# The mLSTM's scores as two pairs of 64-row matmuls in two banks, without the block-diagonal query tile

## The chip, the core and the metric

The kernel runs on one core of a Trainium2 chip. The metric is the device time of one execution in microseconds. Its engines are called as the profile calls them: PE (TensorE, matmuls; PEld are its weight loads), DVE (VectorE), ACT (ScalarE), POOL (GpSimd), SP (SyncE, which here issues DMAs). Each takes its instructions in the order that the program gives it.

## What is computed

One layer of a hybrid encoder, for 1024 prompt frames and 32 sample frames of width 1024: a combined input projection feeds an mLSTM (4 heads of 64), a forgetting attention ("fox", 8 heads) and a spatial gate; their outputs are concatenated ("mix") and projected; then come a layer norm, a SwiGLU feed-forward and a second norm. The change is in the mLSTM, which goes by chunks. Cut to what matters:

```python
def _mlstm_chunk(carry, inp):
    C0, n0, m0 = carry
    q, k, v, li, lf = inp
    ...
    s = jnp.einsum('bthd,bshd->bhts', q, k) * w_intra
    num = (jnp.einsum('bhts,bshd->bthd', s, v)
           + jnp.einsum('bthk,bhkv->bthv', q, C0) * w_inter.transpose(0, 2, 1)[..., None])
    den = s.sum(-1) + jnp.einsum('bthk,bhk->bht', q, n0) * w_inter
    ...
    h = num / den.transpose(0, 2, 1)[..., None]
```

## The kernel before

Everything is float32. The large products split each operand into a high and a low part and run three matmuls of a faster float32 kind (L130 to L132, L402 to L404); the mLSTM's small products are plain float32 matmuls, each of which shows as two weight loads and two matmul rows in the profile.

The mLSTM goes over 9 chunks (`mlstm(j)`): 8 of 128 prompt frames, and the 32 sample frames as chunk 8. A chunk loads `qk` (tag `mqk`): 128 partitions, on which heads 0 and 2 lie in partitions 0 to 63 and heads 1 and 3 in 64 to 127; columns 0 and 1 of its second axis are the queries of the two head pairs, 2 and 3 their keys. For the scores, a tile `qb` (tag `mqb`, one buffer) holds the queries block-diagonally: POOL sets it to zero (L719), two DMAs bring each head's 64 rows into its own half (L722), and one matmul for each pair contracts over all 128 rows and gives two heads side by side (L746), both pairs in one PSUM bank of the pool `pss` (tag `s`). DVE multiplies the bank by the decay weights `mw` (L748). Then follow the transposed keys (L754, a bank of the pool `pt`, tag `t`), the numerator `nd` (L762), the old state's part (L767), the state's update (L777, L784), a chain of small DVE and ACT steps (L793 to L811), and `to_mix` (L821): two PE transposes, a copy by ACT (L823), and a store to `dmix` in DRAM.

PSUM's eight banks are three `g` for the large products, two `t` for transposes (fox's, the keys', `to_mix`'s) and modulation, two `s` for fox's and the mLSTM's scores, and one `o`.

Chunks 0 to 3 are interleaved with fox heads 0 to 7 and the rest of the input projection, by a written list:

```python
ORDER = "q0 f0 g q1 a f1 a g S q2 f2 k1p s a q3 f3 a v q4 f4 a q5 f5 o a m0 G0 q6 f6 a m1 G1p G2p q7 m2 f7 a m3 G3"
```

Fox and mLSTM stand in it under `tc.high_priority(HPA)`. What each engine gets, and in which order, is set by a planner of the language (`schedule_with_timeline_sim=True`), which puts instructions in the order in which it reckons that their operands and buffers will be ready. After this stretch comes the output projection's first half, "wo0": `wo_mix(0, ...)` loads `dmix` (L1130) k tile by k tile, in the order 2, 3, 4, 6, 7, 5, 0, 1, where 0 and 1 are the mLSTM's; ACT and DVE split them (L1131, L1132); `wo_range` runs 24 matmuls for each of 8 output blocks, and DVE adds each to the residual `z` (L1199), which empties its bank. The first block's `z` is also averaged as a pivot (L1056 to L1058). Chunks 4 to 8 run later, among fox's second half and the feed-forward (`mixers`).

The tag `mqb` serves once more, for `scan` in `gates`, before the chunks.

## Time and profile before

| | |
|---|---|
| time, median of 3 runs | 1345.75 us (1345.29 to 1346.57) |
| span of the profiled execution | 1344.9 us |
| PE busy | 1324.0 us, 98% |
| PEld busy | 1208.3 us, 90% |
| DVE busy | 989.1 us, 74% |
| ACT busy | 655.8 us, 49% |
| POOL busy | 231.9 us, 17% |
| DMA, SP's queue | 49.0% of 16 engines |
| granted PE clock | full in all 40 slices (9 of 9 tenths) |

The page gives the profiled execution's span, and no other time of it; the runs' median lies 0.85 us above that span. In a timeline row stand start and length in us, engine, line, operation, output<-inputs by the program's names, shape and count; a bracket tells how long the engine sat idle before and what ended that. Rows of one kind that follow each other are merged. SPq is the issue of a DMA, not its transfer. A matmul's row begins with its stream and ends when its result is out, so rows overlap; the step from one start to the next is what it takes of PE. "128*128" ahead of a shape are the rows and columns of weights.

### The profile page before, as it was taken

To read this page: it belongs to the slowest core of one execution; us is meant where nothing else is said; L and a number is where in the kernel's file an instruction comes from. 1 tells how busy PE (TensorE), PEld (TensorE's weight loads), DVE (VectorE), ACT (ScalarE), POOL (GpSimd) and SP (SyncE) were. 2 spreads that over 40 slices of the span, in tenths; PEclk is the share of its full clock that TensorE was granted. 3 is DMA by queue.
4 is the path that set the end of the run, shared out by engine and by line. 5 is a ranking of instruction groups with operands and counts; after the bars stand their busy time and mean duration, and the time that the engine had idled before them with its cause. 6 is when DMAs were issued, how large, how long until landed. Compare 5 with 4: busy or idle time off the path is not lost.

```text
span 1344.9 us, 25607 instructions
## 1 busy us (share of the span) xinstructions
PE 1324.0 (98%) x9684; PEld 1208.3 (90%) x9684; DVE 989.1 (74%) x2091; ACT 655.8 (49%) x1305; POOL 231.9 (17%) x263
## 2 busy tenths in 40 slices
PE   9999999999999999999999999999999999999996
PEld 6798888888999888888888888999999999999995
DVE  5635655678779667686876776678979887988777
ACT  3413445455547545545454454435754453635355
POOL 0102100143246100000000001464610000000341
PEclk9999999999999999999999999999999999999999
DMA  9585465546557754454344332663785858554221
GB/s 362 207 299 154 150 204 186 174 131 207 181 195 257 191 136 130 117 163 126 115 121 116 110 104 82 217 175 112 205 231 154 228 148 225 139 175 131 89 79 67
DMA packets 119450, 221.73 MB, mean 165 GB/s; under 512 B 18580, under 2 KB 62768, under 8 KB 119328
## 3 DMA queue, kind: packets, MB, share of 16 engines
q1 hardware_dynamic: 112096, 207.55, 49.0%
q0 software_dynamic: 6032, 11.94, 5.2%
q8 instruction: 76, 1.25, 0.4%
q10 hardware_dynamic: 1200, 0.62, 0.2%
q14 instruction: 46, 0.38, 0.1%
HBM read 188.13 MB, written 51.85 MB: 178 GB/s over the span
## 4 chain that ended last, share of the span: by engine, by line
PE 68%; DVE 4%; DMA 1%; ACT 1%; issue 1%; DVEq 0%; ACTq 0%
PE up_g L130 6%; PE up_g L132 6%; PE up_g L131 6%; PE dn_g L130 4%; PE dn_g L132 4%; PE dn_g L131 4%; PE sup_u L132 3%; PE sup_u L131 3%; PE sup_u L130 3%; PE wo_g L131 2%; PE wo_g L132 2%; PE wo_g L130 2%; PE sup_g L132 2%; PE sup_g L131 2%; PE sup_g L130 2%; PE fox_t L943 2%
## 5 line engine op out<-in xcount | busy, mean ns | idle before, releaser
L130 PE MATMUL up_g<-tm_ah,up_whi 128*128 128x512 f32 (+1 forms) x384 | 140.0, 365 | 0.0
L131 PE MATMUL up_g<-tm_al,up_whi 128*128 128x512 f32 (+1 forms) x384 | 140.0, 365 | 0.0
L132 PE MATMUL up_g<-tm_ah,up_wlo 128*128 128x512 f32 (+1 forms) x384 | 139.7, 364 | 0.0
L1368 ACT CAST sup_whi<-sup_raw 128x1024 fp32r<-128x1024 f32 x54 | 56.1, 1048 | 89.3 <-PE dn_u L131 43.9
L130 PEld LDWEIGHTS up_g<-tm_ah,up_whi 128*128 128x128 f32 x384 | 72.3, 188 | 11.1 <-DVE tm_al L1246 0.4
L132 PEld LDWEIGHTS up_g<-tm_ah,up_wlo 128*128 128x128 f32 x384 | 72.3, 188 | 11.1
L131 PEld LDWEIGHTS up_g<-tm_al,up_whi 128*128 128x128 f32 x384 | 72.3, 188 | 10.7
L916 ACT ACTIVATE fox_p<-fox_s,fox_fmx 128x384 f32<-128x384 f32 (+2 forms) x96 | 55.2, 579 | 53.0 <-DVE fox_fmx L914 41.2
L1199 DVE SCALAR_TENSOR_TENSOR wo_z<-dn_g,start_mod,wo_z 128x512 f32<-128x512 f32 (+4 forms) x120 | 60.3, 521 | 22.6 <-PE dn_g L132 22.0
L118 DVE TENSOR_TENSOR up_wlo<-up_raw,up_whi 128x1024 fp32r<-128x1024 f32 x50 | 65.2, 1305 | 15.0 <-ACT up_whi L117 13.7
L1369 DVE TENSOR_TENSOR sup_wlo<-sup_raw,sup_whi 128x1024 fp32r<-128x1024 f32 x54 | 68.0, 1263 | 10.7 <-ACT sup_whi L1368 10.7
L117 ACT CAST up_whi<-up_raw 128x1024 fp32r<-128x1024 f32 x50 | 52.4, 1048 | 47.2 <-PE up_g L131 23.9
L130 PE MATMUL dn_g<-up_acth,dn_whi 128*128 128x512 f32 (+2 forms) x200 | 73.5, 368 | 0.8 <-DVE wo_z L1199 0.8
L132 PE MATMUL dn_g<-up_acth,dn_wlo 128*128 128x512 f32 (+2 forms) x200 | 73.3, 366 | 0.0
L131 PE MATMUL dn_g<-up_actl,dn_whi 128*128 128x512 f32 (+2 forms) x200 | 72.8, 365 | 0.0
L948 ACT CAST fox_pth<-fox_t 128x512 fp32r<-128x512 f32 (+1 forms) x80 | 41.6, 542 | 59.2 <-PE fox_t L943 57.5
L117 ACT CAST dn_whi<-dn_raw 128x1024 fp32r<-128x1024 f32 (+1 forms) x44 | 42.7, 971 | 51.7 <-PE up_g L131 16.0
L911 DVE TENSOR_REDUCE fox_fmx<-fox_s 128x1 f32<-128x384 f32 (+2 forms) x96 | 52.8, 553 | 16.3 <-PE fox_s L908 15.0
L949 DVE TENSOR_TENSOR fox_ptl<-fox_t,fox_pth 128x512 fp32r<-128x512 f32 (+1 forms) x80 | 49.9, 631 | 15.9 <-ACT fox_pth L948 15.6
L118 DVE TENSOR_TENSOR dn_wlo<-dn_raw,dn_whi 128x1024 fp32r<-128x1024 f32 (+1 forms) x44 | 49.5, 1125 | 10.4 <-ACT dn_whi L117 9.5
L402 PE MATMUL tm_g<-tm_whi,start_h1h 128*128 128x256 f32 (+1 forms) x192 | 55.3, 288 | 0.7 <-DVE tm_traw L477 0.7
L1320 POOL DMA_DIRECT2D start_dp<-w_gu x19 | 19.8, 1067 | 209.0 <-DMA start_dp<-w_gu 209.0
(684 smaller groups left out, 4799.7 us busy)
## 6 DMA issues: line engine op xcount, KB each, us to landing
up_raw<-w_gu SPq DMA_DIRECT2D x50, 512.0 KB
ada_late<-w_ada SPq DMA_DIRECT2D x28, 512.0 KB
dn_raw<-w_dn SPq DMA_DIRECT2D x28, 512.0 KB
sup_raw<-w_gu SPq DMA_DIRECT2D x20, 512.0 KB
start_dp<-w_gu SPq DMA_DIRECT2D x19, 512.0 KB
start_dp<-w_gu POOLq DMA_DIRECT2D x19, 512.0 KB, 8.0
wo_raw<-w_o SPq DMA_DIRECT2D x18, 512.0 KB
sup_raw<-start_dp SPq DMA_DIRECT2D x18, 512.0 KB
```

Source lines behind the costliest of these rows:

```text
L117: nc.scalar.copy(hi[:, :w], raw[:, :w])
L118: (eng or nc.vector).tensor_tensor(lo[:, :w], raw[:, :w], f(hi[:, :w]), ALU.subtract)
L130: nc.tensor.matmul(ps, hi, xh(k), start=start and k == 0, stop=False)
L131: nc.tensor.matmul(ps, hi, xl(k), start=False, stop=False)
L132: self.lastmm = nc.tensor.matmul(ps, lo, xh(k), start=False, stop=stop and k == n - 1)
L402: nc.tensor.matmul(ps[:, :ncol], xh, hi, start=k == 0, stop=False)
L911: nc.vector.tensor_reduce(mxs[:, x:x + 1], s[:, :w], AX.X, ALU.max, negate=True)
L916: nc.scalar.activation(pr[:, lo:hi], banks[x][:, :hi - lo], AF.Exp, bias=mxs[:, 0:1], accum_out=sums[:, x:x + 1])
L949: nc.vector.tensor_tensor(pl[:, :e], ps[:, :e], f(ph[:, :e]), ALU.subtract)
L1199: self.lastz = self.nc.vector.scalar_tensor_tensor(z[:, m, x:y], ps[:, x - a:y - a], g[i], z[:, m, x:y], ALU.mult, ALU.add)
L1368: nc.scalar.copy(h, x)
L1369: tt(l, x, f(h), ALU.subtract)
```

## The change

The tile `qb`, its memset and its two DMAs for each chunk go. Each head's score is now a matmul of its own, contracted over the head's 64 rows: queries and keys of one head lie on the same partitions of `qk`. Heads 0 and 2 (rows 0 to 63) go to a bank of `pss`, heads 1 and 3 (rows 64 to 127) to a bank of `pt`. DVE's product with the weights becomes two, one for each bank. The scan of `gates` gets a tag of its own.

```diff
-        scan = t([R, 2, 192], "mqb")
+        scan = t([R, 2, 192], "mscan")
...
-        qb = t([P, 2, 2, P], "mqb")
-        nc.gpsimd.memset(qb, 0.0)
-        for a in range(2):
-            r = slice(64 * a, 64 * a + 64)
-            self.load(qb[r, :, a, :L], self.dmqk[r, 0:2, o:o + L])
...
-        st = self.t(self.pss, [P, 512], F32, "s")
+        sts = [self.t(p, [P, 512], F32, x) for p, x in ((self.pss, "s"), (self.pt, "t"))]
         for i in range(2):
-            nc.tensor.matmul(st[:L, 256 * i:256 * i + 256].rearrange("p (a q) -> p a q", a=2)[:, :, :L],
-                             qk[:, 2 + i, :L], qb[:, i, :, :L], start=True, stop=True)
-        nc.vector.tensor_tensor(w[:L, :, :L], st[:L].rearrange("p (h q) -> p h q", h=4)[:, :, :L], w[:L, :, :L], ALU.mult)
+            for a, st in enumerate(sts):
+                r = slice(64 * a, 64 * a + 64)
+                nc.tensor.matmul(st[:L, P * i:P * i + L], qk[r, 2 + i, :L], qk[r, i, :L], start=True, stop=True)
+        for a, st in enumerate(sts):
+            wa = w.rearrange("p (i a) q -> p i a q", a=2)[:L, :, a, :L]
+            nc.vector.tensor_tensor(wa, st[:L, :256].rearrange("p (i q) -> p i q", i=2)[:, :, :L], wa, ALU.mult)
```

Lines behind the change have numbers lower by 2 in the changed kernel (L821 is L819, L1132 is L1130); the scores are its L743.

The planner makes another order of it. PE at chunk 0's scores, before (`tm_g` are the projection's products; the number at a name's end tells tiles apart):

```order
L403 MATMUL tm_g_559_3096<-tm_wlo_550_2970,start_ah_53_169 128x256
L404 MATMUL tm_g_559_3096<-tm_whi_549_2969,start_al_54_170 128x256
L746 MATMUL mlstm_s_580_3280<-mlstm_mqb_575_3259,mlstm_mqk_574_3257 128x256 x2
L402 MATMUL tm_g_561_3124<-tm_whi_546_2963,start_h1h_55_171 128x256
L403 MATMUL tm_g_561_3124<-tm_wlo_547_2964,start_h1h_55_171 128x256
```

PE at the same place after, and 123 matmuls on, where the other half stands (`ada_t` is a modulation product on groups of 32 columns):

```order
L404 MATMUL tm_g_559_3096<-tm_whi_549_2969,start_al_54_170 128x256
L743 MATMUL mlstm_s_579_3276<-mlstm_mqk_574_3257 128x128 x2
L402 MATMUL tm_g_561_3124<-tm_whi_546_2963,start_h1h_55_171 128x256
...
L404 MATMUL tm_g_567_3208<-tm_whi_549_2969,start_h1l_56_172 128x256
L202 MATMUL ada_t_571_3240<-ada_late_570_3238,start_c32_62_182 32x256
L743 MATMUL mlstm_t_580_3277<-mlstm_mqk_574_3257 128x128 x2
L202 MATMUL ada_t_571_3240<-ada_late_570_3238,start_c32_62_182 32x256 x3
```

The two pairs of a chunk stand apart. Counted in PE's whole order, there are 123, 99, 74, 136, 57, 21, 0, 24 and 27 other matmuls between the two pairs in chunks 0 to 8; in chunk 4 the s pair is itself cut in two. The program gives 64-row matmuls a form of their own (64x128 weights), which before the change only the four transposes of L687 in `gates` had.

PE where chunk 3's output goes to the mix, before (`mlstm_t_826` are its two transposes, `fm_g` the input projection's products):

```order
L130 MATMUL fm_g_868_4786<-start_h1h_55_171,fm_whi_862_4748 128x272
L131 MATMUL fm_g_868_4786<-start_h1l_56_172,fm_whi_862_4748 128x272
L821 MATMUL mlstm_t_826_4432<-start_ident_40_120,mlstm_mhm_820_4412 128x128 x2
L132 MATMUL fm_g_868_4786<-start_h1h_55_171,fm_wlo_863_4749 128x272
L130 MATMUL fm_g_868_4786<-start_h1h_55_171,fm_whi_862_4748 128x272
```

PE there after (`wo0_g` 892, 897 and 902 are the output projection's first three blocks, each with its own bank):

```order
L131 MATMUL wo0_g_902_5002<-tm_al_849_4652,wo0_whi_900_4998 128x256
L132 MATMUL wo0_g_902_5002<-tm_ah_848_4651,wo0_wlo_901_4999 128x256
L819 MATMUL mlstm_t_826_4432<-start_ident_40_120,mlstm_mhm_820_4412 128x128 x2
L130 MATMUL wo0_g_892_4927<-tm_ah_848_4651,wo0_whi_890_4923 128x256
L130 MATMUL wo0_g_897_4964<-tm_ah_848_4651,wo0_whi_895_4960 128x256
L130 MATMUL wo0_g_902_5002<-tm_ah_848_4651,wo0_whi_900_4998 128x256
```

The transposes moved from among the input projection's products to behind 54 of the output projection's; the row behind them is that projection's k tile 0. DVE in chunk 3's chain, after (`mlstm_mmu` is the head norm's mean, `tm_al` the low half of the projection's k tile 5, which holds fox heads 6 and 7; before, no `tm_al` stood between L800 and L811):

```order
L796 TENSOR_TENSOR mlstm_mhm_820_4412<-mlstm_mtot_816_4395,mlstm_mden_819_4408 128x256
L798 TENSOR_REDUCE mlstm_mmu_821_4414<-mlstm_mhm_820_4412 128x4
L1130 TENSOR_TENSOR tm_al_849_4652<-tm_al_849_4652,tm_ah_848_4651 128x512
L799 TENSOR_SCALAR mlstm_mmu_821_4414<-mlstm_mmu_821_4414 128x4
L782 SCALAR_TENSOR_TENSOR fm_C_392_2220<-fm_C_392_2220,fm_d0c_394_2224,mlstm_s_818_4401 64x65 x4
L800 TENSOR_TENSOR mlstm_mhm_820_4412<-mlstm_mhm_820_4412,mlstm_mmu_821_4414 128x256
L118 TENSOR_TENSOR wo0_wlo_901_4999<-wo0_raw_899_4996,wo0_whi_900_4998 128x1024
```

The split of k tile 5 moved to between two steps of the chain. On SP, chunk 3's store to the mix and the two loads of k tiles 0 and 1 are followed by six loads of the residual `z` before the next weights of the projection; before, the loads of `z` came in groups of 1, 2, 3 and 2 among other issues.

## The prediction

> **What bounds the kernel now.** I read the page first, then PE's waits, then the tiles of the mLSTM scores, then the timelines of the two places where the changed order differs most.

> ```profile
> span 1344.9 us, 25607 instructions
> PE 1324.0 (98%) x9684; PEld 1208.3 (90%) x9684; DVE 989.1 (74%) x2091; ACT 655.8 (49%) x1305; POOL 231.9 (17%) x263
> ```

> ```profile
> PE start_o L294 <- DVE start_onesm L161: 1.2, 1, 1.2
> PE fox_o L951 <- DVE fox_ptl L949: 1.1, 1, 1.1
> PE tm_g L848 <- DMA tm_gvn<-start_dvn: 0.4, 1, 0.4
> ```

> TensorE (PE) sets the time: it is busy 98% of the span, and its longest single wait is 1.2 us. So what lengthens or empties PE's queue is paid in full, and what shortens DVE, ACT, POOL or the DMA queues is worth nothing unless PE waits for it. The sums below are made against this execution's span, 1344.9 us; the median of the runs, 1345.75, lies 0.85 above it, and I let that stay.

> ```profile
> L746 PE MATMUL mlstm_s<-mlstm_mqb,mlstm_mqk x36: 219/379/382, 239.9 to 716.4; 128*128 128x256 f32 x32, 128*32 128x64 f32 x4
> L748 DVE TENSOR_TENSOR mlstm_mw<-mlstm_s,mlstm_mw x9: 271/692/693, 242.1 to 717.0; 128x512 f32<-128x512 f32 x8, 32x128 f32<-32x128 f32 x1
> ```

> A float32 matmul shows as two passes, so a chunk's two score matmuls are four rows of L746.

> **The score matmuls themselves.**

> ```profile
> 239.83 0.28 PE L404 MATMUL tm_g<-tm_whi,start_al 128*128 128x256 f32 x1
> 239.95 1.03 PE L746 MATMUL mlstm_s<-mlstm_mqb,mlstm_mqk 128*128 128x256 f32 x4
> 240.63 0.47 PE L402 MATMUL tm_g<-tm_whi,start_h1h 128*128 128x256 f32 x1
> 240.93 0.28 PE L403 MATMUL tm_g<-tm_wlo,start_h1h 128*128 128x256 f32 x1
> ```

> ```profile
> 353.69 0.45 PE mlstm_s L777 x4
> 346.66 1.00 PE ada_t L202 x16
> ```

> From 239.95 to 240.93 PE does four L746 passes and one tm_g pass (0.12, the step from 239.83 to 239.95): 0.98 - 0.12 = 0.86 us a chunk. After, it does eight passes with 128 columns. Nearest is L777 (128 weights, 130 columns): four passes in 0.45, so eight in 0.90. One after the other they cost 8 x 0.04 = 0.3 us more. Two at a time would save 0.45 a chunk. L202 shows that PE can do it on column groups: 16 passes of 256 columns in 1.00 us, where four L746 passes of that width take 0.86. But the order of the changed program keeps the two row groups apart: the pair for bank s and the pair for bank t have 21 to 136 other matmuls between them in eight chunks, and are neighbours in chunk 6 alone. So I take +0.3, with ends -3.6 (all eight paired) and +0.3.

> [...]

> **Going in and out of the 64-row form.**

> ```profile
> 174.64 0.28 PE L402 MATMUL tm_g<-tm_whi,start_ah 128*128 128x256 f32 x1
> 174.85 0.25 PE L687 MATMUL gates_t<-start_ident,gates_mw 36*128 36x36 f32 x1
> 175.03 0.39 PE L403 MATMUL tm_g<-tm_wlo,start_ah 128*128 128x256 f32 x1
> 175.25 0.29 PE L404 MATMUL tm_g<-tm_whi,start_al 128*128 128x256 f32 x1
> 175.38 0.28 PE L402 MATMUL tm_g<-tm_whi,start_ah 128*128 128x256 f32 x1
> 175.59 0.31 PE L687 MATMUL gates_t<-start_ident,gates_mw 36*128 36x36 f32 x2
> 175.83 0.39 PE L403 MATMUL tm_g<-tm_wlo,start_ah 128*128 128x256 f32 x1
> 176.05 0.28 PE L404 MATMUL tm_g<-tm_whi,start_al 128*128 128x256 f32 x1
> ```

> L687 holds 36 rows, and the program gives it the 64x128 form that the new scores have. From 174.64 to 175.25 there are two tm_g passes (0.24) and one L687: 0.61 - 0.24 = 0.37. With two L687 it is 0.67 - 0.24 = 0.43, so the second costs 0.06 and the trip out and back costs about 0.30. The changed order has 18 groups of 64-row matmuls (chunks 0 to 8: 2, 2, 2, 2, 3, 2, 1, 2, 2). Two border column-tiled groups that changed form anyway, or replace chunk 8's old one: 16 new trips, 16 x 0.30 = +4.8 us. Ends: 0 (hidden behind the longer passes) and 18 x 0.37 = 6.7. Chunk 0's t pair stands inside a set of four L202 column groups and leaves one alone: two L746-like passes of 0.215, +0.4.

> [...]

> **The loads, the memset and DVE.** Gone are 18 DMA issues on SP, 9 memsets on POOL and their wait for the previous chunk's scores. No PE wait in the list above is behind them: 0, ends -1.1 (the fox_o wait, if DVE comes earlier) and 0. DVE's product is split in two, 0.69 to about 2 x 0.42 (the halves as wide as L810, below): +0.15 x 9 on an engine that is 74% busy; the mLSTM chain has PE's other matmuls as cover, except in chunk 3.

> **Chunk 3 in front of the output projection.** The t pair now comes late: chunk 3's comes 138 matmuls after its s pair, and its transposes to the mix (L821, after: L819) come behind 54 matmuls of the output projection, whose three banks are by then filled up to k 5. The next PE row is that projection's k 0, which needs these very transposes by way of ACT, a store, a load and ACT. Before, 88 matmuls lay between:

> ```profile
> 357.87 0.38 PE L821 MATMUL mlstm_t<-start_ident,mlstm_mhm 128*128 128x128 f32 x2
> 358.59 0.36 ACT L823 COPY mlstm_mtot<-mlstm_t 128x256 f32<-128x256 f32 x1
> 359.13 0.39 SPq L91 DMA_DIRECT2D start_dmix<-mlstm_mtot  x1
> 362.52 0.80 SPq L87 DMA_DIRECT2D tm_al<-start_dmix  x2
> 365.35 0.62 ACT L1131 CAST tm_ah<-tm_al 128x512 fp32r<-128x512 f32 x1 [2.03 <-DMA tm_al<-start_dmix]
> 366.91 0.28 PE L130 MATMUL wo_g<-tm_ah,wo_whi 128*128 128x256 f32 x1
> 369.04 0.28 PE L130 MATMUL wo_g<-tm_ah,wo_whi 128*128 128x256 f32 x1
> ```

> The operand is ready at 365.35 + 0.62 = 365.97, 8.1 us after L821, and PE wants it at 369.04, 18 matmuls after the projection's first at 366.91: 3.1 us to spare. After, PE has only the two transposes (0.2) for these 8.1. The store's landing took 3.4 here; fox's took 2.3:

> ```profile
> 351.85 0.67 DVE L963 TENSOR_TENSOR fox_fo<-fox_o,fox_fo 64x512 f32<-64x512 f32 x1
> 352.55 0.46 SPq L91 DMA_DIRECT2D start_dmix<-fox_fo  x1
> 354.86 0.33 SPq L87 DMA_DIRECT2D tm_al<-start_dmix  x1
> 357.68 0.62 ACT L1131 CAST tm_ah<-tm_al 128x512 fp32r<-128x512 f32 x1 [1.44 <-DMA tm_al<-start_dmix]
> 358.33 0.69 DVE L1132 TENSOR_TENSOR tm_al<-tm_al,tm_ah 128x512 fp32r<-128x512 f32 x1 [0.81 <-ACT tm_ah L1131]
> ```

> So PE waits 6.8 to 7.9 us; I take 7.5, nearer the same transfer.

> The transposes themselves may be late. On DVE the low half of k 5 (L1132) now stands ahead of the chain's mean, and it ends 6.5 us after the last fox head's L963 ends (352.52 to 359.02).

> ```profile
> 353.45 0.42 DVE L810 TENSOR_TENSOR mlstm_mhm<-mlstm_mhm,mlstm_mrs 128x256 f32<-128x256 f32 x1
> 354.18 1.17 DVE L784 SCALAR_TENSOR_TENSOR fm_C<-fm_C,fm_d0c,mlstm_s 64x65 f32<-64x65 f32 x4 [0.31 <-PE mlstm_s L777]
> 355.76 1.23 DVE L118 TENSOR_TENSOR wo_wlo<-wo_raw,wo_whi 128x1024 fp32r<-128x1024 f32 x1
> ```

> From the t pair: L963 ends about 3.1 us later (five fox matmuls, ACT, DVE), L1132 at 9.6, then C (1.17), a weight split (1.23), five steps near 0.42 and eight of 0.15 to 0.5: about 6.4, so 16.0. PE gets to the transposes after the pair itself (0.7) and 114 matmuls (0.12 each, a few twice that): 14.8. Wait 1.2, ends 0 and 4.

> Then the three banks end together. The first is emptied at once (0.4 lost to pivot and hand-over); the second's L1199 stands on DVE behind a weight split and the pivot:

> ```profile
> 372.03 0.48 DVE L1199 SCALAR_TENSOR_TENSOR wo_z<-wo_g,start_mod,wo_z 128x256 f32<-128x256 f32 x1
> 373.42 1.05 ACT L117 CAST wo_whi<-wo_raw 128x1024 fp32r<-128x1024 f32 x1 [3.15 <-DMA wo_raw<-w_o]
> 377.94 0.48 DVE L1199 SCALAR_TENSOR_TENSOR wo_z<-wo_g,start_mod,wo_z 128x256 f32<-128x256 f32 x1
> ```

> Before, the second came 5.9 us after the first. After, SP issues that weight behind six residual loads, so I keep 5.9; meanwhile PE has the fourth output block (24 x 0.12) and the pivot (0.43), 3.3 in all. Lost about 2.2, ends 0 and 5.

> **Sum.** 0.3 + 4.8 + 0.4 + 0 + 7.5 + 1.2 + 0.4 + 2.2 = 16.8 us, so a span of 1361.7 and a time of 1362.5.

> **Rivals.** (1) Only the bare transfer is paid: transposes on time, no wait for banks, a store as quick as fox's: 5.5 + 6.8 = 12.3, 1358. For it: DMA queues are emptier while PE waits. Against: the DVE rows above are in order. (2) Form changes are free: 16.8 - 4.8 = 12.0, also 1358; L687 speaks against it, though its passes are shorter. (3) Chunks 0 to 3 lose more: scores hold a bank of the transposes' pool, and each t pair brings a wait like fox_o's 1.1: 4 x 1.1 more, 1367. The wait list shows it once already; against it, PE's order leaves many matmuls between. (4) Not slower: the pairs overlap after all, place the scores, price -3.6, about 1342. It decides only if the copy, store, load and cast fit in under 3.6 us, where they take 8.1. (5) The change does not do what it says, since the pairs stand apart; that is in the forecast already.

> **How the numbers follow.** The forecast has 0.47, (1) 0.18, (2) 0.11, (3) 0.17, (4) 0.02; 0.05 is left for a small difference either way. The range 1353 to 1369 holds the first four with the ends of the stall; (4) is left out. About 0.2% (2.7 us) is what a measurement can tell from no change: faster 0.03, same 0.03, slower 0.94.

> **What would show it.** Right: the 64-row passes about 0.11 apart, one row group after the other, with 0.3 lost around each group; a PE gap of 7 to 8 us between the transposes to the mix and the projection's k 0, charged to ACT's cast or the tm_al load; a shorter gap before the fifth output block. Wrong: no such gap, scores of both row groups starting a few ns apart, or new waits in the fox stretches larger than these.

## The result and the profile after

The changed kernel takes 1370.04 us (median of 4 runs, 1364.53 to 1373.32) against 1346.16 for the kernel before in the same measurement (1345.29 to 1346.85): a ratio of 1.0178, 95% interval 1.0161 to 1.0196. It is slower by 24 us, where 16.8 were forecast, and the median lies 1 us above the top of the range. The runs themselves differ by 9 us, which those of the kernel before do not.

The head of the page, then PE's longest waits (in all, times, longest, in us):

```profile
span 1362.7 us, 25635 instructions
...
PE 1332.1 (98%) x9720; PEld 1212.2 (89%) x9720; DVE 990.9 (73%) x2100; ACT 656.6 (48%) x1305; POOL 227.7 (17%) x254
```

```profile
PE wo_g L130 <- ACT tm_ah L1129: 5.9, 1, 5.9
PE wo_g L130 <- DVE wo_z L1197: 2.1, 1, 2.1
PE tm_g L402 <- ACT tm_brs L462: 1.9, 1, 1.9
PE tm_g L402 <- ACT tm_vhl L837: 1.7, 1, 1.7
...
PE mlstm_t L819 <- DVE mlstm_mhm L809: 0.6, 1, 0.6
```

The profiled execution is the fastest of the four (1364.53). PE is busy 8.1 us longer, and beside the wait of 1.2 us at the start and smaller ones there are four new ones of 1.7 to 5.9. The first two are those of the forecast, the third and fourth were not in it.

The score matmuls, and DVE's product, now one for each bank:

```profile
L743 PE MATMUL mlstm_s<-mlstm_mqk x36: 192/272/374, 239.6 to 735.7; 64*128 64x128 f32 x32, 64*32 64x32 f32 x4
...
L743 PE MATMUL mlstm_t<-mlstm_mqk x36: 192/272/373, 255.8 to 729.1; 64*128 64x128 f32 x32, 64*32 64x32 f32 x4
```

```profile
L746 DVE TENSOR_TENSOR mlstm_mw<-mlstm_s,mlstm_mw x9: 204/415/425, 241.1 to 736.6; 128x256 f32<-128x256 f32 x8, 32x64 f32<-32x64 f32 x1
```

PE's timeline at chunk 0's first pair, and at chunk 6, the one chunk in which the two pairs are neighbours:

```profile
239.35 0.28 PE L404 MATMUL tm_g<-tm_whi,start_al 128*128 128x256 f32 x1
239.56 0.71 PE L743 MATMUL mlstm_s<-mlstm_mqk 64*128 64x128 f32 x4
240.20 0.39 PE L402 MATMUL tm_g<-tm_whi,start_h1h 128*128 128x256 f32 x1
240.42 0.28 PE L403 MATMUL tm_g<-tm_wlo,start_h1h 128*128 128x256 f32 x1
```

```profile
631.19 0.37 PE L743 MATMUL mlstm_t<-mlstm_mqk 64*128 64x128 f32 x1
631.21 0.37 PE L743 MATMUL mlstm_s<-mlstm_mqk 64*128 64x128 f32 x1
631.40 0.27 PE L743 MATMUL mlstm_t<-mlstm_mqk 64*128 64x128 f32 x1
631.42 0.27 PE L743 MATMUL mlstm_s<-mlstm_mqk 64*128 64x128 f32 x1
...
631.64 0.27 PE L743 MATMUL mlstm_s<-mlstm_mqk 64*128 64x128 f32 x1
631.84 0.50 PE L905 MATMUL fox_s<-fox_k,fox_qp 128*128 128x512 f32 x1
```

From 239.35 to 240.42 lie two tm_g passes (0.117 each) and one group of four: 1.07 - 0.23 = 0.84 us, of which four passes at 0.112 are 0.45. The trip out and back is 0.39. A chunk has two such groups, 1.68 us where the four wide passes took 0.86. In chunk 6 eight passes go from 631.19 to 631.84, 0.65 us, as long as four take elsewhere (239.56 to 240.20): the two row groups start about 14 ns apart and run side by side. In the kernel with neighbours and the new list below, the rows of a t and an s pass start 0.00 to 0.01 us apart (514.60 to 515.04).

The timeline at chunk 3's transposes to the mix (L819), answering to the rows of L821 to L130 before:

```profile
378.17 0.42 DVE L809 TENSOR_TENSOR mlstm_mhm<-mlstm_mhm,mlstm_mo 128x256 f32<-128x256 f32 x1
...
378.74 0.41 PE L819 MATMUL mlstm_t<-start_ident,mlstm_mhm 128*128 128x128 f32 x2 [0.62 <-DVE mlstm_mhm L809]
379.18 0.37 ACT L821 COPY mlstm_mtot<-mlstm_t 128x256 f32<-128x256 f32 x1 [2.20 <-PE mlstm_t L819]
...
379.58 0.37 SPq L91 DMA_DIRECT2D start_dmix<-mlstm_mtot  x1
...
381.42 0.80 SPq L87 DMA_DIRECT2D tm_al<-start_dmix  x2
...
384.39 0.62 ACT L1129 CAST tm_ah<-tm_al 128x512 fp32r<-128x512 f32 x1 [2.00 <-DMA tm_al<-start_dmix]
...
385.06 1.01 PE L130 MATMUL wo_g<-tm_ah,wo_whi 128*128 128x256 f32 x3 [5.91 <-ACT tm_ah L1129]
...
386.17 0.41 PE L132 MATMUL wo_g<-tm_ah,wo_wlo 128*128 128x256 f32 x1
...
386.38 0.41 PE L130 MATMUL wo_g<-tm_ah,wo_whi 128*128 128x256 f32 x1
```

The gap is where it was forecast and has the cause that was named. But behind it the projection's matmuls stand 0.21 us apart (386.17 to 386.38), nearly twice the usual 0.117: the granted clock has fallen to 0.50. Stretches cut at the clock's own borders show it. First the columns, then the changed kernel in the execution above, then a second execution of the same kernel (the run after_rep below); the column behind POOL is the granted clock:

```profile
core 0: us, PE busy (x) PEld busy (x) DVE busy (x) ACT busy (x) POOL busy (x), PEclk, DMA share, GB/s
274.10:277.52 3.42, 2.37 (x11) 1.41 (x9) 3.42 (x6) 0.00 (x0) 2.81 (x2) 1.00 0.70 186
277.52:280.93 3.41, 2.59 (x22) 2.62 (x23) 2.75 (x6) 3.35 (x8) 1.73 (x3) 1.00 0.24 83
...
379.92:383.33 3.41, 0.00 (x0) 0.00 (x0) 2.80 (x3) 2.47 (x3) 0.00 (x0) 1.00 0.39 98
383.33:386.74 3.41, 1.68 (x7) 1.67 (x8) 2.08 (x3) 1.24 (x2) 0.00 (x0) 0.50 0.93 293
386.74:390.16 3.42, 3.42 (x16) 3.22 (x15) 0.48 (x1) 0.00 (x0) 0.00 (x0) 0.50 1.05 358
390.16:393.57 3.41, 3.01 (x25) 2.81 (x23) 0.81 (x1) 1.89 (x3) 0.47 (x1) 1.00 1.05 396
```

```profile
276.40:279.81 3.41, 1.54 (x12) 1.14 (x11) 3.17 (x9) 1.83 (x7) 1.86 (x3) 1.00 0.46 151
279.81:283.22 3.41, 3.41 (x18) 3.41 (x18) 2.30 (x3) 3.33 (x5) 2.67 (x3) 0.50 0.65 177
334.42:337.84 3.42, 1.74 (x13) 1.32 (x12) 3.36 (x12) 3.10 (x7) 0.00 (x0) 1.00 1.06 372
337.84:341.25 3.41, 3.41 (x19) 3.41 (x18) 2.99 (x11) 0.76 (x3) 0.00 (x0) 0.50 0.31 86
```

In these two executions the clock falls to half and rises only at borders 3.41 us apart: in the first at 383.33, two steps on at 390.16, and 285 steps behind the first border at 1356.13; in the second at 279.81, 283.22, 337.84, 341.25, 385.62 and 392.45. In the profiled execution of the kernel before, its records have it at half from 1338.3 us to the end of the span and nowhere else; single runs of that kernel on other chips reach 1349.5 and 1350.6 us at a mean clock of 0.995, so it may lose a window now and then, but none of those was profiled. In the first execution after, it is at half for two windows behind the gap, in which PE works 1.68 + 3.42 us: 2.55 us lost. In the second execution two more windows are lost, behind a wait of 1.9 us at 277 and a pair of 0.8 and 0.9 at 335. Waits of about that sum are there in the first execution too (1.9, and 0.6 with 1.7), but they lay across borders: of the two windows that the one at 276 touches, PE was busy 2.37 and 2.59 us, of the two at 335 it was busy 2.08 and 2.43, and the clock stayed.

### The profile page after: what moved, and what is told of

It is laid out like the page before. It is cut to its first block, busy times and chain, and to the rows that moved or that the text cites. A ratio compares the mean times of both kernels' runs of the same rounds, so it can differ in the third digit from the quotient of the medians.

```text
span 1362.7 us, 25635 instructions
## 1 busy us (share of the span) xinstructions
PE 1332.1 (98%) x9720; PEld 1212.2 (89%) x9720; DVE 990.9 (73%) x2100; ACT 656.6 (48%) x1305; POOL 227.7 (17%) x254
## 4 chain that ended last, share of the span: by engine, by line
PE 72%; DVE 4%; DMA 2%; ACT 1%; issue 1%; SPq 0%; DVEq 0%; ACTq 0%
PE up_g L132 6%; PE up_g L130 6%; PE up_g L131 6%; PE dn_g L130 4%; PE dn_g L132 4%; PE dn_g L131 4%; PE sup_u L132 3%; PE sup_u L131 3%; PE sup_u L130 3%; PE wo_g L130 2%; PE wo_g L132 2%; PE wo_g L131 2%; PE sup_g L131 2%; PE sup_g L132 2%; PE sup_g L130 2%; PE fox_t L941 2%
## 5 line engine op out<-in xcount | busy, mean ns | idle before, releaser
L130 PE MATMUL up_g<-tm_ah,up_whi 128*128 128x512 f32 (+1 forms) x384 | 140.4, 366 | 0.0
L130 PEld LDWEIGHTS up_g<-tm_ah,up_whi 128*128 128x128 f32 x384 | 72.3, 188 | 11.0 <-issue 0.4
L117 ACT CAST up_whi<-up_raw 128x1024 fp32r<-128x1024 f32 x50 | 52.4, 1048 | 55.6 <-PE up_g L131 28.7
L118 DVE TENSOR_TENSOR up_wlo<-up_raw,up_whi 128x1024 fp32r<-128x1024 f32 x50 | 65.0, 1300 | 15.8 <-ACT up_whi L117 14.6
L130 PE MATMUL dn_g<-up_acth,dn_whi 128*128 128x512 f32 (+2 forms) x200 | 73.4, 368 | 0.0
L117 ACT CAST dn_whi<-dn_raw 128x1024 fp32r<-128x1024 f32 (+1 forms) x44 | 42.7, 971 | 51.4 <-PE up_g L131 17.8
L402 PE MATMUL tm_g<-tm_whi,start_ah 128*128 128x256 f32 (+1 forms) x192 | 55.1, 288 | 2.0 <-ACT tm_brs L462 1.9
L402 PE MATMUL tm_g<-tm_whi,start_h1h 128*128 128x256 f32 (+1 forms) x192 | 55.3, 288 | 1.7 <-ACT tm_vhl L837 1.7
L404 PE MATMUL tm_g<-tm_whi,start_h1l 128*128 128x256 f32 (+1 forms) x192 | 54.8, 285 | 0.0
```

The costliest lines, as they stand in the source:

```text
L117: nc.scalar.copy(hi[:, :w], raw[:, :w])
L118: (eng or nc.vector).tensor_tensor(lo[:, :w], raw[:, :w], f(hi[:, :w]), ALU.subtract)
L130: nc.tensor.matmul(ps, hi, xh(k), start=start and k == 0, stop=False)
L402: nc.tensor.matmul(ps[:, :ncol], xh, hi, start=k == 0, stop=False)
L404: self.lastmm = nc.tensor.matmul(ps[:, :ncol], xl, hi, start=False, stop=k == 7)
```

## The experiments

Where nothing else is said, a ratio is to the kernel before on the same chip, with its 95% interval.

**Work in the gap.** Only the filler is added; PE's order is otherwise the same.

```diff
+        late = self.t(self.po, [P, 512], F32, "o")
+        for _ in range(24):
+            x = nc.tensor.matmul(late[:, :P], self.onesm, self.onesm, start=True, stop=True).ins
...
```

> The changed kernel with 24 extra float32 matmuls (128 weights, 128 columns, into the bank of the pool po, nobody reads them) that stand on TensorE between chunk 3's two transposes to the mix and the output projection's k tile 0; all else stands in the same order. They take 24 x 2 x 0.112 = 5.4 us of the 6.1 us gap. Theory (the gap costs its own length and then a stretch of half clock whose length differs from run to run): the operand is ready no sooner, so the gap's 6.1 us stay, but there are no records at half clock ahead of the kernel's end; 1361 to 1363 us, all runs within 1.5 us. Rival (the spread from 1364.5 to 1373.3 us and the lower mean clock come from elsewhere, say from the 64-row form): median near 1370, spread of some 9 us as in the changed kernel.

Measured: 1367.8 us (1365.84 to 1370.22), 1.0170 (1.0152 to 1.0187). PE now waits 0.4 us ahead of k tile 0, and no half clock follows, but four other windows fell to half, behind waits of 1.8 to 2.1 us at 235, 279 and 399 us and a pair of 0.8 and 0.7 at 338. So neither theory held as it was put: the gap's two windows can be filled away, yet the spread was not the gap's alone. The theory became: any window with enough idle time is followed by one at half clock, and where the borders lie differs from run to run. The spans agree with it: 1367.4 less 4 windows of 1.7 is 1360.6; the first execution above, 1362.7 less 2.55, is 1360.1.

**The second bank without the 64-row form.** The kernel before, its two head pairs in two banks.

```diff
+        sts = [self.t(p, [P, 512], F32, x) for p, x in ((self.pss, "s"), (self.pt, "t"))]
+        for i, st in enumerate(sts):
+            nc.tensor.matmul(st[:L, :256].rearrange("p (a q) -> p a q", a=2)[:, :, :L],
                              qk[:, 2 + i, :L], qb[:, i, :, :L], start=True, stop=True)
...
```

> The kernel before, with its block-diagonal query tile and its 128-row matmuls, but the second head pair's scores go to a bank of the pool pt (tag t) and DVE's product is two. No 64-row form. Theory (the bank of the transposes' pool makes the second pair, and with it chunk 3's chain, late; this is most of the loss): the gap ahead of the output projection's k tile 0 is there (its transposes come 54 matmuls behind the projection's first, as in the changed kernel), so 6.1 + 2.3 + 0.8 us and a stretch at half clock of 2.5 to 9 us: 1357 to 1364. Rival (the 64-row form itself is the loss, by its trips and by what they do to the clock): 1346 to 1348.

Measured: 1364.31 us (1362.42 to 1365.95), 1.0138 (1.0121 to 1.0156), just above the top of the theory's range. The gap is there with 5.7 us, the fifth block's bank with 3.1, waits of 1.8 and 2.0 near 276 and 335, and five windows at half clock. A second bank from the transposes' pool, with DVE's product in two, thus brings most of the loss (18.6 of 24 us) without the 64-row form.

**Neighbours.** The changed kernel, a chunk's four matmuls chained.

```diff
...
+            self.chained([mms[x] for x in (((0, 1), (0, 0), (1, 1), (1, 0)) if j < 6 else ((0, 0), (0, 1), (1, 0), (1, 1)))])
```

> The changed kernel with each chunk's four score matmuls chained in the order t, s, t, s (s, t, s, t from chunk 6 on), so that they stand next to each other in all nine chunks. Chunk 3's transposes still come behind 54 to 64 of the projection's matmuls. Theory (neighbours of different row groups run side by side, as chunk 6 showed, and there is one trip per chunk): a chunk costs 0.39 + 4 x 0.112 = 0.84 us in place of about 1.68, so 8 chunks x 0.84 = 6.7 us less than the changed kernel: median about 1363, and a gap with a half clock as before it. Rival (alternating instructions of two row groups don't overlap, each in its turn): 0.39 + 8 x 0.112 = 1.29 a chunk, so 3 us less: 1367.

Measured: 1368.52 us (1367.69 to 1369.03), 1.0174 (1.0158 to 1.0189). The overlap came in all nine chunks: in a full chunk eight passes, first start to last start, take 0.443 us, where four apart took 0.437. The time did not follow: neither 1363 nor the rival's 1367. In chunk 0 the s pair now stands at 255.9 us, where the t pair was, and no longer at 239.6; I take it that a pair held back for its second bank makes the chains behind it late. PE waits for them, and five windows run at half clock:

```profile
PE wo_g L130 <- ACT tm_ah L1138: 5.7, 1, 5.7
PE mlstm_t L828 <- DVE mlstm_mhm L818: 3.9, 1, 3.9
PE wo_g L130 <- DVE wo_z L1206: 2.7, 1, 2.7
PE mlstm_s L784 <- DVE mlstm_mtot L775: 2.6, 1, 2.6
```

**The written list, three kernels.** In each, chunks 1 to 3 stand one place earlier; it is tried on the changed kernel, on the changed kernel with neighbours, and on the kernel before.

```diff
-... a m0 G0 q6 f6 a m1 G1p G2p q7 m2 f7 a m3 G3"
+... a m0 G0 m1 q6 f6 a m2 G1p G2p q7 m3 f7 a G3"
```

> The changed kernel with chunks 1 to 3 one place earlier in the written list (m1 ahead of q6, m2 ahead of G1, m3 ahead of f7). The pairs still stand apart and there are as many trips, but chunk 3's transposes now come 104 matmuls ahead of the output projection. Theory (loss = trips + the late chain): no gap ahead of k tile 0, no half clock; what is left is 16 x 0.39 + 0.3 + 0.4 and some 1.5 us of small waits: 1353 to 1356. Rival (the late chain of chunk 3 is only where a loss shows that the chunks bring anyway; the wait moves elsewhere): above 1362.

> The changed kernel with both edits: the four score matmuls of a chunk are neighbours (t, s, t, s), and chunks 1 to 3 stand one place earlier in the written list. Chunk 3's transposes come 110 matmuls ahead of the output projection. Theory (trips, waits and the clock are all of the loss): one trip a chunk, so 0.84 us a chunk against 0.86 before; no gap ahead of k tile 0; what is left are small waits for the bank of the transposes' pool: 1347 to 1352. Rival (making a pair wait for two banks costs as many waits as it saves): 1356 or more, with waits of 2 us and half-clock windows behind them.

> The kernel before, with chunks 1 to 3 one place earlier in the written list, and nothing else: the control for the two kernels that have that list. Theory (the list alone costs nothing, since the kernel before has no wait there): 1344 to 1348. Rival (the list itself brings waits that were read as the change's): 1350 or more.

Measured: 1359.78 us (1.0103, 1.0081 to 1.0126), 1357.00 (1.0079, 1.0057 to 1.0101) and, for the control, 1356.43 (1.0071, 1.0043 to 1.0099). The theory missed on all three; the second and the control lie where their rivals had them. The list alone costs 10 us in the kernel before, where it makes waits of its own:

```profile
PE mlstm_t L821 <- DVE mlstm_mhm L811: 3.2, 1, 3.2
PE tm_g L402 <- DVE tm_traw L477: 2.6, 1, 2.6
```

So these kernels don't tell what chunk 3's late chain is worth. Nor are their waits the control's. With neighbours, PE waits 4.9 us for another k tile, the one that is loaded behind the store of the last fox output (PE's last matmul ahead of the wait starts at 371.13):

```profile
368.79 0.45 SPq L91 DMA_DIRECT2D start_dmix<-fox_fo  x1
372.13 0.33 SPq L87 DMA_DIRECT2D tm_al<-start_dmix  x1
375.61 0.62 ACT L1138 CAST tm_ah<-tm_al 128x512 fp32r<-128x512 f32 x1 [3.19 <-DMA tm_al<-start_dmix]
376.28 1.01 PE L130 MATMUL wo_g<-tm_ah,wo_whi 128*128 128x256 f32 x3 [4.87 <-ACT tm_ah L1138]
```

Against that control, neighbours are 0.6 us slower on the same chip, and pairs apart some 4 us by the ratios; the intervals overlap, so neither is told from nothing.

**Both banks from the scores' pool.**

```diff
-        sts = [self.t(p, [P, 512], F32, x) for p, x in ((self.pss, "s"), (self.pt, "t"))]
+        sts = [self.t(p, [P, 512], F32, x) for p, x in ((self.pss, "s"), (self.pss, "s"))]
```

> The changed kernel with both banks of the scores from the pool pss, so that the transposes' pool is as before. The pairs stand 7 to 27 matmuls apart in chunks 0 to 3, and stand together in chunks 7 and 8; chunk 3's transposes come 36 matmuls ahead of the projection's first. Theory (the transposes' bank made the chain late): 14 trips x 0.39 = 5.5 us and a shorter gap ahead of k tile 0 (54 + 36 matmuls of 0.12 before it, against 8.1 us of copy, store, load and cast: no gap): 1351 to 1355. Rival (it is any second bank that makes the chain late, here fox's): 1360 or more.

Measured: 1357.82 us (1354.62 to 1363.79), 1.0089 (1.0055 to 1.0123), between the two ranges. The gap at k tile 0 is gone, as the theory had it, but the projections' waits of 2.9 and 3.0 are new. The profile is of the fastest run and has no window at half clock ahead of the kernel's end; the runs differ by 9 us.

**A trip by itself.** The kernel before, with one 64-row group more ahead of each chunk's scores.

```diff
+        extra = [nc.tensor.matmul(st[:L, P * i:P * i + L], qk[0:64, 2 + i, :L], qk[0:64, i, :L], start=True, stop=True).ins
+                 for i in range(2)]
```

> The kernel before, with one more group of two 64-row matmuls ahead of each chunk's scores (heads 0 and 2 alone, into the same bank, overwritten by the scores behind it); nothing waits for it. It adds 9 trips into the 64-row form and 9 x 4 passes. Theory (a trip costs 0.39 us of PE's time, as the spacing in the changed kernel's trace says): 9 x (0.39 + 4 x 0.112) = 7.5 us: 1353 to 1354, no wait above 1.5 us and no new record of half clock. Rival (the spacing hides behind the weight loads, or PE catches up): 9 x 0.45 = 4.0 us: 1349 to 1350.

Measured: 1352.34 us (1351.49 to 1355.06), 1.0049 (1.0034 to 1.0065): 6.6 us (4.6 to 8.7). The rival's 4.0 lies outside, the theory's 7.5 inside, though the median is 0.7 below the 1353 that was forecast. The trace has ten groups and not nine, since chunk 4's is cut in two, and the passes take 3.7 us (chunk 8's are short). Put down to the trips alone, the rest is 0.29 us for each (0.09 to 0.50).

**The late transposes alone, with and without filler.** The kernel before, its chunk 3's L821 held behind the first 54 matmuls of the projection; in the second kernel the 24 filler matmuls stand in the gap.

```diff
+            if a == 0 and m == 2:
+                pe = [i for i in nc.cur_bb.bb.instructions[first:] if i.engine == mybir.EngineType.PE]
+                for y in self.mix3:
+                    self.tc.add_manual_dep(y, pe[17].name, mybir.DependencyInfo(
...
```

> The kernel before, with chunk 3's two transposes to the mix held behind the first 54 matmuls of the output projection, where the changed kernel has them; scores, query tile and all other chunks as before. Theory (a gap costs its length, and then half-clock windows of 3.41 us): 6.1 us for the gap, 2.3 for the fifth block's bank, and 2 to 3 windows at half clock, 2.5 to 4.2 us: 1357 to 1359, mean clock 0.993 to 0.995. Rival (the clock is a trait of the 64-row form, and the gap costs its length alone): 1354 to 1355, mean clock 0.997.

> The same kernel (chunk 3's transposes held behind 54 matmuls of the projection), with 24 float32 matmuls that nobody reads in the gap between these transposes and k tile 0. Nothing else differs. Theory: the operand comes no sooner, but PE is busy 5.4 us of the gap and no half-clock window follows: 2.5 to 3.4 us less than without the 24, 1354 to 1356, mean clock 0.996 or more. Rival (work in the gap makes no difference, the clock falls by itself): the same time as without them, within 1 us.

Measured: 1360.41 us (1357.09 to 1364.71), 1.0103 (1.0088 to 1.0117), and with filler 1355.03 (1352.42 to 1356.83), 1.0071 (1.0057 to 1.0085). The first lies 1.4 above its theory's range, the second inside. The gap's window and the one behind it, without filler (first two rows) and at the same place with it (last two; columns as above):

```profile
380.32:383.73 3.41, 0.00 (x0) 0.00 (x0) 3.00 (x3) 1.64 (x3) 0.00 (x0) 1.00 0.56 161
383.73:387.14 3.41, 3.02 (x13) 3.01 (x14) 1.39 (x2) 0.96 (x2) 0.00 (x0) 0.50 0.97 313
...
380.11:383.52 3.41, 2.88 (x22) 2.47 (x22) 1.68 (x3) 1.24 (x2) 0.00 (x0) 1.00 0.92 287
383.52:386.93 3.41, 3.30 (x26) 3.05 (x25) 1.39 (x3) 0.39 (x1) 1.54 (x2) 1.00 1.06 384
```

This pair parts the gap's length from its clock. But the 5.4 us between the medians, where 2.5 to 3.4 were expected, are not the gap's window alone: with filler the planner orders ACT and DVE differently behind the gap, the bank's wait is 3.4 us without it and 1.8 with it, and without it three other windows fell as well, one behind a wait at 237 us, before anything the edit moves. With filler, the two runs whose mean clock was 0.998 took 1352.4 and 1352.9, some 7.5 us above the kernel before: the gap (5.7 without filler) and the bank (1.8). The three at 0.995, below the 0.996 expected, took 1355.0 to 1356.8; in the profiled one a window fell behind the bank's wait. Without filler, the mean clock was 0.992 to 0.995. Here half clock came without the 64-row form and without the second bank, behind the gap of 5.7 us, and with filler the gap's window (PE busy 2.88 of 3.41 us) brought none.

**Nine equal waits.** The kernel before, with a chain of ACT copies between blocks of the feed-forward's second half, for which PE has to wait (a hold); three copies, then eight.

```diff
+        nc.scalar.copy(x, p[:, :32])
+        for _ in range(2):
+            nc.scalar.copy(x, x)
+        q = self.t(self.pt, [P, 512], F32, "t")
+        d = nc.tensor.matmul(q[:, :32], self.onesm, x, start=True, stop=True).ins
...
```

> The kernel before, with nine holds in the feed-forward's second half: behind a block, a small matmul of 32 columns waits for a chain of three ACT copies of 32 columns that begins at the block's end, and all later matmuls stay behind it. Each holds PE for an estimated 1.1 to 1.5 us. Theory (a wait of less than half a window of 3.41 us never brings half clock): 9 x (1.1 to 1.5) = 10 to 14 us and nothing more: 1356 to 1360, no half-clock record in that stretch. Rival (any wait over 1 us can bring it): up to 9 x 1.7 = 15 us more.

> The kernel before, with the same nine holds made longer: eight ACT copies in a chain, an estimated 2.2 to 2.8 us each. Theory (a window that stands idle for half of its 3.41 us or more is followed by one at half clock, wherever the window's borders happen to lie): 9 x 2.5 = 22 us for the waits, and some 6 of the 9 are followed by a window at half clock, 6 x 1.7 = 10 us: 1375 to 1382, with runs some us apart. Rival (half clock needs a whole idle window of 3.41 us): 22 us alone, 1366 to 1371, no half-clock record in that stretch.

Measured: 1374.14 us (1369.95 to 1375.82), 1.0211 (1.0194 to 1.0228), and 1391.49 (1390.61 to 1392.25), 1.0345 (1.0330 to 1.0359). Both are beyond the ranges. The holds are longer than I put them, 15.4 and 27.0 us in all, with each hold's matmul on top; and more windows fell than forecast, three where the theory had none and ten where it had six, which the traces price at 5.1 and 16.3 us (half of PE's work in them). So a wait of 1.6 us, less than half of 3.41, was followed by half clock, against the first theory, and so were eight of the nine longer holds, 3.0 us each on average and less than a whole window, against the second rival. The shorter holds show both outcomes: in six of the nine PE waits alike (1.6 us), and yet two of them bring a window at half clock and four do not. Two stretches of the first kernel, the window with the hold and the one behind it:

```profile
1133.95:1137.36 3.41, 1.81 (x14) 1.60 (x14) 1.80 (x4) 1.56 (x4) 0.00 (x0) 1.00 0.86 111
1137.36:1140.77 3.41, 3.41 (x17) 3.41 (x16) 1.76 (x3) 0.00 (x0) 0.00 (x0) 0.50 0.24 43
...
1144.19:1147.60 3.41, 1.81 (x15) 1.79 (x15) 1.76 (x3) 1.50 (x4) 0.00 (x0) 1.00 0.10 11
1147.60:1151.01 3.41, 3.41 (x29) 3.41 (x28) 1.28 (x4) 0.00 (x0) 0.00 (x0) 1.00 0.37 143
```

PE was busy 1.81 us in both windows, and only the first is followed by half clock: at 1.81 of 3.41 us PE's busy time alone does not decide. What else does stays open. Of the nine longer holds (2.8 us and more) eight brought half clock; the ninth lay across a border.

**The change by chunks.** New scores in chunks 4 to 8 alone, in chunks 0 to 3 alone, and in all but chunk 3.

```diff
+        new = j > 3
+        if not new:
+            qb = t([P, 2, 2, P], "mqb")
...
```

(`j < 4` and `j != 3` in the other two.)

> The new scores in chunks 4 to 8 alone; chunks 0 to 3 keep the block-diagonal tile, and the order up to the output projection is the one before. Theory (trips are paid in full, and nothing else happens there): 9 more trips x 0.39 = 3.5 us: 1348.5 to 1350.5, no wait above 1.5 us behind chunk 4, no half-clock record ahead of the kernel's end. Rival (the second bank makes waits there too): 1353 or more.

> The new scores in chunks 0 to 3 alone; chunks 4 to 8 keep the block-diagonal tile. Theory: all of the loss but 3.5 us is here, 7 trips (2.7) + 0.4 + the late chain (7.7 with its bank) + small waits (some 3) + half clock (3 to 7): 1363 to 1368. Rival (trips and waits are spread evenly over nine chunks): 1346 + 24 x 4/9 = 1357.

> The changed kernel, with chunk 3 alone back on the block-diagonal tile. Chunk 3's transposes then come 11 matmuls ahead of the projection's first, 65 ahead of its k tile 0, some 7.8 us of work against the 8.1 us that their way takes. Theory (chunk 3's late chain and the half clock behind it are half of the loss): no gap over 1 us at k tile 0; 1370 less 6.1, 2.3, 0.8 and 3 to 6 of half clock: 1355 to 1359. Rival (the other chunks make their own waits and windows): 1362 or more.

Measured: 1349.26 us (1.0030, 1.0018 to 1.0041), 1365.28 (1.0144, 1.0128 to 1.0159) and 1359.44 (1.0108, 1.0090 to 1.0126). Chunks 4 to 8 cost 4.0 us (2.4 to 5.5), with no half clock: 0.44 a trip (0.27 to 0.61) if all of it is put down to their nine trips. Chunks 0 to 3 cost 20. Both are as the theory had them. Without chunk 3 some 9 us of the 24 are gone by the ratios, and the median lies 0.4 above the range given: k tile 0 waits 0.9 us, but the bank's wait (2.5) and the one at 276 (1.9) stay.

**The changed kernel again.**

> The changed kernel once more, unchanged, for a second profile of it. Theory (its runs differ by how many waits of 1.7 us or more fall inside one window of the clock): the same PE order and nearly the same waits; the span is 1360.1 us and 1.7 for each half-clock window that PE works through, so with three more windows than in the first profile some 5 us longer. Rival (runs differ by the length of the waits): the same two windows, and a longer gap ahead of k tile 0.

Measured: 1367.53 us, span 1365.8, with the same order on PE, two more windows at half clock than in the first execution, not three, and the gap ahead of k tile 0 at 5.7 (5.9 there). Its half-clock windows hold 3.41 + 3.41 + 2.22 + 3.41 us of PE's work (the third and fourth are 385.62 to 392.45), half of which is 6.2: 1365.8 - 6.2 = 1359.6, against 1360.1 in the first. Without the clock the two executions are the same within 0.5 us.

**Neighbours in chunks 4 to 8 alone.** As the first of the three above, with the chain of neighbours.

> As late_new (new scores in chunks 4 to 8 alone), with the four score matmuls of a chunk chained as neighbours in alternating order. Theory (neighbours run side by side: eight passes take 0.443 us, as four did, and there is one trip in and out): 0.84 us a chunk against 0.86 before, so the 4 us of late_new are given back: 1344.5 to 1347, no difference from the kernel before that can be measured, and no gain. Rival (the trip is paid as often, or the pair's wait for its second bank costs what the trip saves): 1348 to 1351.

Measured: 1348.63 us (1346.19 to 1350.99), 1.0023 (1.0014 to 1.0031); the rival's range. PE's busy time is back (1324.3 us, 1324.0 before, 1326.5 with pairs apart), but there is a new wait ahead of the second half's projection; that the later pairs delay the chain it needs is my reading, and half of the 3 us is left open:

```profile
PE wo_g L130 <- ACT up_ah L1159: 1.6, 1, 1.6
```

No kernel here beats the one before, and none points to one that would: with neighbours eight passes cost what four wide ones did, so there is nothing to gain on PE, and qb's loads and memset were hidden: no PE wait of the kernel before stood behind them.

## Why the prediction was wrong

**The missing step: the clock.** The sum put it at nothing, and gave no reason. The kernel before shows full clock in all 40 slices, and I let that stand for the changed kernel, in which I forecast an idle stretch of 7.5 us. A span of 1361.7 was forecast; without the clock the two profiled executions come to 1360.1 and 1359.6. The clock adds 2.55 and 6.2 us in them. The slowest runs show a mean clock of 0.991 where the fastest has 0.995: 0.004 x 1371 = 5.5 us (rounding allows 1.4 either way) of the 7 to 9 us between them; they were not profiled, and the rest stays open. The median, 1370.04, lies 7.5 us above the forecast time, and the profiled execution, which lost two windows alone, lies 2 above it. That half clock came behind waits in these kernels is shown by the pair with and without filler, and by the nine holds.

The other steps:

- Streaming, +0.3: right. The passes stand 0.112 apart, and the pairs are neighbours in chunk 6 alone.
- Trips, 16 x 0.30: too small. 0.39 in the trace, so 6.2 us; the whole-kernel runs give 0.29 and 0.44 with intervals that hold both values, and so can't tell them apart. L687's 0.30 was for passes of 36 columns; why groups of 128 columns lose more was not tested.
- Loads, memset, DVE at nothing: no wait after speaks against it, and POOL's and DVE's totals changed by under 5 us without PE following.
- Chunk 3's wait, 7.5: 5.9 and 5.7, below the lower end of 6.8. Store and loads landed sooner than fox's row led me to take: from the last transposes to k tile 0's operand it is 385.0 - 378.7 = 6.3 us, where 8.1 was taken from the place in the kernel before.
- Transposes late, 1.2: 0.6.
- The fifth block's bank, 0.4 + 2.2: 2.1.
- Rival (3), that chunks 0 to 3 lose more because a pair holds a bank of the transposes' pool: it happened in part, as waits of 1.9 and 1.7 where it had four of 1.1, and the forecast's sum left them out; the kernel with two banks and no 64-row form has them too. Which DVE or ACT step makes each late was not followed further.
- Rivals (2) and (4): trips are not free (0.39 us), and row groups do overlap (14 ns apart in chunk 6), but here only where they are neighbours.
- Rival (1), only the bare transfer is paid: its quick store came true, and the gap is shorter still than its 6.8, but the late transposes and the bank's wait are there too.

So place, cause and sign of the gap were right, and the size missed by the clock. That the rest comes so near, 15.2 us in the first execution without the clock against 16.8, is in part luck. Trips came out 1.4 too small and the gap 1.6 too large; the two new waits of 3.6 were left out, and so were waits of the kernel before that grew shorter: PE's idle time grew by 9.7 us, while its five new waits make 12.2.

## What to carry to other kernels

Before pricing a new PE wait by its length, add the clock: in these runs waits of 1.6 to 2.1 us on an otherwise full PE were followed in part by a window of 3.41 us at a granted clock of 0.50, by estimate another 1.7 us, half of that window (its matmuls stood 0.21 us apart, at full clock 0.117). Whether a window followed depended in part on where the wait fell: the one of 1.9 us near 276 lost none in the changed kernel's first execution and one in its second. The changed kernel's runs lay 9 us apart. When a tile gets a second bank from a pool that others use, look for the chain behind that pool and where its last step then stands in PE's order; the second bank, and not the matmuls, was most of this loss, and chunk 3's chain some 9 of the 24 us. Small matmuls on different row groups ran side by side here only as neighbours in PE's order (eight passes in 0.65 us, as long as four elsewhere), and a trip into their form took 0.39 us, nearly as much as four of their passes (0.45).

## What the runs showed of the hardware

The trips. Of the 0.39 us, some 0.09 to 0.11 is lost at each of four steps: ahead of the first 64-row pass, behind it, ahead of the first wide pass after, and behind that. At chunk 0's s pair these steps are 0.210, 0.214, 0.202 and 0.223 us, where 0.117, 0.112, 0.112 and 0.117 are usual.
